# Attention on one core: the order of all engines as a table in the source, in place of a forward model

## The chip, the cores and the metric

The kernel runs on one core of a Trainium2 chip. Its time is the device time of one execution in microseconds; 113.61 us is the median of three executions before the change (113.47 to 114.02). A profile was taken of one more execution.

Engines are named as the profile names them: PE is TensorE (PEld its weight loads), DVE is VectorE, ACT is ScalarE, POOL is GpSimd, SP is SyncE, which here only issues transfers. Each engine works off its own queue in order; between engines there are semaphores.

## The reference

Plain softmax attention over 8 x 8 heads of 512 positions by 64:

```python
def reference(q, k, v):
    scale = 1.0 / np.sqrt(q.shape[-1])
    scores = np.einsum('bhqd,bhkd->bhqk', q, k) * scale
    scores = scores - scores.max(axis=-1, keepdims=True)
    attn = np.exp(scores)
    attn = attn / attn.sum(axis=-1, keepdims=True)
    return np.einsum('bhqk,bhkd->bhqd', attn, v).astype(np.float32)
```

q, k and v are (8, 8, 512, 64) in float32, normally distributed.

## The kernel before

**Tiling.** The 64 heads are taken two at a time: 32 pairs g, with the heads h = 0 and 1 (a and b below). A pair's q, k and v are loaded by one transfer of 256 KB each into float32 tiles, seven tiles deep for each of the three. POOL casts them to fp16 (`cast`, lines 511 to 526): v into one of twelve buffers with a column of ones, q and k into one of five `qkp` tiles. For pair 1's q alone the cast is shared: VectorE does the first half of it (line 523) and POOL the second (line 524).

**Stages of a pair.** TensorE turns k and q round in two halves (`transposes`, line 550; the part 0 is k, the part 1 is q), and VectorE copies the result from PSUM into `tqk` (`copy`). For pair 1 each half has a copy of its own (line 565), and the copy of the key half is issued inside `transposes`, at its end (line 560); for all other pairs one copy serves both halves (line 571). Then come the scores: a group m is two blocks of 128 keys by 512 queries in one of three score banks (`scores`, line 576, matmuls on line 598). There are 129 groups, four to a pair, with the last one cut in two halves. ScalarE takes the exponential of a group in one activation of 128 x 1024 (line 602). Sixteen groups (`ON_DVE`) are not given to ScalarE: VectorE computes their exponential with a "raise" out of the score bank (line 625) and five "passes" in SBUF (lines 642 to 665, called passes 0 to 4 here). Such a raise frees the score bank, which the group three further on takes.

**Values.** A value unit is a product of 128 queries of one head with its four blocks of keys (`values`, line 696, matmuls on line 704), with 65 columns: the last is the sum for the division. Seven units share a bank of PSUM. VectorE takes reciprocals of the sums (line 671) and multiplies (line 676) into a ring of 112 units, from which SP stores one or two heads at a time (lines 690 and 694). The two PSUM banks x0 and x1 are shared by the units and the transposes.

**What sets the order.** The kernel is written with a manual schedule: whatever the source issues first for an engine comes first in that engine's queue. The class `Plan` (lines 18 to 426) is a forward model: it steps a clock by 5 ns, keeps modelled times for each engine, the PSUM banks, the loads and the port that VectorE's passes and POOL's casts share, and by rules of urgency picks the next step of each engine. `run` returns the steps in the order of modelled time, and a loop at the end of the kernel issues them. Two things are added as waits: `cast_behind` (line 539) makes a cast wait for an earlier VectorE instruction, counted back from the latest one (`behind`), and before a cast of k a POOL memset of one number waits for transposes five pairs back. Twelve activations (`KNOWN`) wait for a cast six casts back.

The first pair is issued by hand (`first_pair`), ahead of the modelled steps: its activations are those on line 801.

Of the kernel before, what the change touches and what calls it, by code (L numbers as in the profile page):

```python
# [17 lines left out]
class Plan:  # L18

    SLOT, EXP, EXP_DONE, EXP_FIXED = 216, 853, 181, 64  # L20
    INTO, OUT_OF = 96, 96
    TRANSPOSE, V_UNIT = 222, 128
    TO_ACT, TO_DVE, TO_PE = 220, 210, 60

    COPY, NORM, RAISE = (601, 690), (50, 133), (1132, 1215)
    RECIPROCAL = 115
    SCALE, PRODUCT, EXTRA = 333, 600, 29
    COPY_1 = (400, 190)
    NORM_COLUMN, PASS_DONE = 67, 115
    PASSES = (SCALE, SCALE, PRODUCT, SCALE, PRODUCT)  # L30
    BITS = 2
    NEEDS = (None, None, 0, 2, 3)
    FIRST_EXP = 5000
    STEP = 5
    CALM, KEEN = 9000, 4
    FIRST_UNIT = 4
    KNOWN, OVER = (13, 15, 18, 20, 22, 24, 27, 42, 50, 61, 69, 97), 6
    ON_DVE = (5, 10, 16, 25, 28, 39, 44, 54, 63, 66, 74, 81, 91, 96, 103, 116)

    LATE_NORM, LATE_COPY, HURRY, SOON, BACKLOG = 700, 1500, 800, 160, 600  # L40
    LATE_MUL, WAIT = 400, 200
    SLACK, AHEAD = 0, 2

    CAST, CAST_PORT, CAST_DONE, TO_POOL = 557, 475, 130, 150
    SCALE_PORT, PRODUCT_PORT, GAP, REACH = 271, 537, 20, 5
    FIRST_LAND, LOAD, STORE, LATENCY, ISSUE = 5200, 752, 376, 2300, 470
    QUEUED, URGENT = 3500, 16
    PAIRED, STORE_ISSUE = 18, 520
    RAW, QK16, NV, NU = 7, 5, 12, 112
    PAIR, DUEK, DUEV, DUEL, PRE = 3300, 3550, 6000, 5000, 0  # L50

    def __init__(self, groups, pairs, first):
        self.groups, self.pairs = groups, pairs
        self.pe, self.act, self.dve = 7000, self.FIRST_EXP, 6300
        self.pool, self.port, self.dma = 4600, 4600, self.FIRST_LAND
        self.m, self.tiled = first, True
        self.read = []
        self.exps = {}
        for m in range(first):
            self.act += self.EXP + self.EXP_FIXED  # L60
            self.exps[m] = self.act + self.EXP_DONE
            self.read.append(self.exps[m])
        self.tq = {0: 5800}
        self.transposed = {0: 5800}
        self.next_t = 1
        self.part_t = 0
        self.banks = [5100, 5800]
        self.todo = [(g, h) for g in range(pairs) for h in range(2)]
        self.last = self.todo.pop()
        self.last_part = 0  # L70
        self.head = None
        self.units = self.FIRST_UNIT
        self.member = {b: m for m, grp in enumerate(groups) for b in grp}
        self.ready = []
        self.passes = []
        self.passed = {}
        self.raised = set()
        self.steps = []
        self.busy_dve = 0
        self.order, self.paired = [], 0  # L80

        late = {grp[0][0] for m, grp in enumerate(groups) if m in self.ON_DVE}
        due = []
        for g in range(pairs):
            scores = 5000 + self.PAIR * g
            if g:
                due += [(scores - self.DUEK, g, "k"), (scores - self.DUEK + 10, g, "q")]
            due.append((scores + self.DUEV + (self.DUEL if g in late else 0), g, "v"))
        self.due = sorted(due)
        self.uncast = list(self.due)  # L90
        self.casts = []
        self.landed, self.cast_done = {}, {}
        self.first_loads = [(g, n) for _, g, n in self.due if g < self.RAW]
        self.first_loads += [(self.RAW, "k"), (self.RAW, "q")]
        for x in self.first_loads:
            self.dma += self.LOAD
            self.landed[x] = self.dma
        self.loads, self.stores, self.stored = [], [], []
        self.sp = 1650 + 470 * len(self.first_loads)

    def note(self, t, *what):
        self.steps.append((t, len(self.steps)) + what)

    def trigger(self, t):

        ops = self.ops
        if not ops or ops[-1][1] <= t - 300:  # L110
            return 1, None
        n = len(ops) - 1
        while (
            n > 0
            and len(ops) - n < self.REACH
            and not ops[n][2]
            and ops[n][0] - ops[n - 1][1] <= self.GAP
        ):
            n -= 1
        if n > 0 and ops[n][0] - ops[n - 1][1] <= self.GAP:  # L120
            n -= 1
        return len(ops) - n, ops[n][1]

    def emit(self, t, back, after):
        _, g, n = self.uncast.pop(0)
        shared = (g, n) == (1, "q")
        self.note(t, "cast", g, n, back if t > self.CALM else 0)
        if not shared:
            self.casts.append((g, n, t if after is None else after + self.TO_POOL))
        if g + self.RAW < self.pairs:  # L130
            self.loads.append((g + self.RAW, n))

    def fits(self, t, soon=0):
        if not self.uncast:
            return False
        _, g, n = self.uncast[0]
        if n != "v" and g >= self.QK16 and self.transposed.get(g - self.QK16, 1e9) > t:
            return False
        return self.landed.get((g, n), 1e9) <= t + soon

    def step_pool(self, t):
        if self.uncast and self.uncast[0][1:] != (1, "q") and not self.casts and self.pool <= t:
            quiet = not self.passes and self.port <= t and not any(x[1] == "raise" for x in self.ready)
            if self.fits(t) and (quiet or self.uncast[0][0] - self.PRE < t):
                self.emit(t, 1, None)
        if self.casts and self.pool <= t and self.port <= t:
            g, n, after = self.casts[0]
            if after <= t and self.landed.get((g, n), 1e9) <= t:
                self.casts.pop(0)
                begin = max(self.pool, self.port, after, self.landed[(g, n)])  # L150
                self.pool = begin + self.CAST
                self.port = begin + self.CAST_PORT
                self.cast_done[(g, n)] = begin + self.CAST + self.CAST_DONE

    def step_sp(self, t):
        if self.sp > t or (self.loads and self.dma > t + self.QUEUED):
            return
        urgent = len(self.stores) > self.URGENT
        if self.loads and not urgent:
            g, n = self.loads[0]  # L160
            if self.cast_done.get((g - self.RAW, n), 1e9) <= t:
                self.loads.pop(0)
                self.note(t, "load", g, n)
                self.dma = max(self.dma, t + self.LATENCY - self.LOAD) + self.LOAD
                self.landed[(g, n)] = self.dma
                self.sp = t + self.ISSUE
                return
        if self.stores and self.stores[0] <= t:
            both = self.both()
            if both and (len(self.stores) < 2 or self.stores[1] > t):  # L170
                return
            heads = 2 if both else 1
            self.note(t, "store", heads)
            self.dma = max(self.dma, t + self.LATENCY - heads * self.STORE) + heads * self.STORE
            for _ in range(heads):
                self.stores.pop(0)
                self.stored.append(self.dma)
            self.paired += heads - 1
            self.sp = t + self.STORE_ISSUE

    def both(self):

        n = len(self.stored)
        g, h, u = self.order[n]
        return (
            self.paired < self.PAIRED
            and g < self.pairs - 2
            and h == 0
            and n + 1 < len(self.order)
            and self.order[n + 1][0] == g  # L190
            and u % self.NU + 8 <= self.NU
        )

    def room(self, t, u):
        heads = (u - self.NU - self.FIRST_UNIT + 3) // 4
        return heads <= 0 or len(self.stored) >= heads and self.stored[heads - 1] <= t

    def free(self, n=0):
        m = self.m + n
        if m >= len(self.groups):  # L200
            return 1e9
        g = self.groups[m][0][0]
        return max(0 if m < 3 else self.read[m - 3], self.tq.get(g, 1e9))

    def for_dve(self, m):
        return m in self.ON_DVE
# [692 lines left out]
```

## Time and profile before

| | us |
|---|---|
| median of the three executions | 113.61 |
| the profiled execution, whole | 113.92 |
| its span (first to last instruction) | 112.1 |
| ACT busy | 105.5 |
| PE busy | 103.2 |
| DVE busy | 100.8 |
| POOL busy | 65.9 |

The profile is of one execution, on the one core. A busy time is the union of an engine's instructions. The text quotes these views: the page's busy shares; the stage view (a stretch of time, its length, and for each engine its busy time and number of instructions, then the granted clock, the DMA share and GB/s); the list of waits (who waited for whom, us in total, how often, the longest); and the timeline (start in us, duration in us, engine, line, operation, what it writes and reads, and in brackets the idle time of the engine before it and what ended it). The line numbers are those of the kernel before.

In short: ScalarE, VectorE and TensorE are all busy for nine tenths of the time. Loads run at about 350 GB/s up to 80 us.

### The profile page before, as it was taken

The numbers are of one execution on the slowest core, as the hardware profiler recorded it, in microseconds if no ns is written. First come the engines' busy times: TensorE is split into PE (matmuls) and PEld (weight loads), VectorE is DVE, ScalarE is ACT, GpSimd is POOL, SyncE is SP. The second block draws the span as 40 slices with busy tenths as digits, with TensorE's granted clock in tenths as the row PEclk, the third lists the DMA queues.
The fourth block names the chain that finished last, engine by engine and source line by source line (L and its number), as shares of the span: only waits on it lengthen the run. The fifth ranks groups of instructions, "written<-read, shape, count | busy, mean of one in ns | idle before, by whom it ended". The sixth has DMA issues, their size and how long they took to land.

```text
span 112.1 us, 4408 instructions
## 1 busy us (share of the span) xinstructions
PE 103.2 (92%) x1728; PEld 69.4 (62%) x1728; DVE 100.8 (90%) x227; ACT 105.5 (94%) x118; POOL 65.9 (59%) x127
## 2 busy tenths in 40 slices
PE   7978889999799998999989999899999999999980
PEld 7634555766367766658647767577557577675660
DVE  1647999999999999999999999999999999997390
ACT  4599999999999999999999999999999999999970
POOL 2147768549756886495594786876784855600000
PEclk9999999999999999999999999999999999999997
DMA  3999999999999999999999999999999974142354
GB/s 106 276 359 353 345 350 347 355 336 349 345 347 336 341 346 343 354 364 375 370 358 382 350 355 377 354 372 362 343 366 305 349 245 143 52 141 99 97 167 161
DMA packets 35093, 33.84 MB, mean 302 GB/s; under 512 B 2304, under 2 KB 35072, under 8 KB 35072
## 3 DMA queue, kind: packets, MB, share of 16 engines
q1 hardware_dynamic: 34496, 33.04, 90.4%
q10 hardware_dynamic: 576, 0.52, 1.4%
q8 instruction: 13, 0.21, 0.8%
q14 instruction: 8, 0.07, 0.2%
HBM read 25.17 MB, written 8.39 MB: 299 GB/s over the span
## 4 chain that ended last, share of the span: by engine, by line
DVE 39%; PE 24%; DMA 15%; issue 8%; POOL 7%; SPq 3%; ACT 2%; POOLq 0%; ACTq 0%
PE o L704 13%; DMA v<-in_v_dram 10%; PE st L598 8%; DVE pd L625 8%; DVE tqk L571 7%; DVE ring L676 7%; DMA q<-in_q_dram 5%; DVE m L659 4%; POOL qkp L525 4%; DVE pd L665 4%; POOL vp L515 3%; PE tp L558 2%; SPq L509 2%; DVE m L642 2%; DVE pe L651 2%
## 5 line engine op out<-in xcount | busy, mean ns | idle before, releaser
L602 ACT ACTIVATE pt<-st 128x1024 f16<-128x1024 f32 (+1 forms) x110 | 100.3, 1144 | 0.2 <-PE st L598 0.2
L704 PEld LDWEIGHTS <-pt 128*128 128x128 f16 x880 | 38.8, 98 | 12.1 <-issue 10.2
L704 PE MATMUL o<-vp,pt 128*128 128x65 f16 x880 | 45.3, 194 | 0.4 <-POOL vp L515 0.2
L598 PE MATMUL st<-tqk 64*128 64x512 f16 (+1 forms) x250 | 41.7, 380 | 2.6 <-ACT pt L602 1.4
L525 POOL CAST qkp<-k 128x512 f16<-128x512 f32 x31 | 22.2, 717 | 11.3 <-DVE rc L671 5.3
L525 POOL CAST qkp<-q 128x512 f16<-128x512 f32 x30 | 21.7, 725 | 9.0 <-DVE rc L671 5.3
L515 POOL CAST vp<-v 128x512 f16<-128x512 f32 x32 | 21.4, 679 | 9.2 <-PE st L598 2.4
L676 DVE TENSOR_TENSOR ring<-o,rc 128x448 f32<-128x448 f32 (+2 forms) x37 | 22.3, 606 | 0.4
L704 PE MATMUL o<-vp,pe 128*128 128x65 f16 x128 | 21.8, 194 | 0.0
L704 PE MATMUL o<-vp,pd 128*128 128x65 f16 x128 | 21.7, 192 | 0.0
L558 PE MATMUL tp<-ident,qkp 128*128 128x128 f16 x248 | 19.6, 220 | 1.6 <-DVE tqk L571 0.8
L558 PEld LDWEIGHTS <-qkp 128*128 128x128 f16 x248 | 14.4, 97 | 9.9 <-issue 4.6
L571 DVE COPY tqk<-tp 128x1024 f16<-128x1024 f16 x30 | 20.3, 683 | 0.0
L625 DVE TENSOR_SCALAR pd<-st 128x1024 uint16<-128x1024 f32 x16 | 19.5, 1216 | 0.7 <-PE st L598 0.7
L598 PEld LDWEIGHTS <-tqk 64*128 64x128 f16 x250 | 10.7, 93 | 11.8 <-issue 4.6
L704 PEld LDWEIGHTS <-pe 128*128 128x128 f16 x128 | 12.5, 98 | 3.4 <-issue 3.3
L704 PEld LDWEIGHTS <-pd 128*128 128x128 f16 x128 | 12.5, 98 | 0.0
L659 DVE TENSOR_TENSOR m<-m 128x1024 f16<-128x1024 f16 x16 | 11.0, 685 | 0.0
L665 DVE TENSOR_TENSOR pd<-pd,m 128x1024 f16<-128x1024 f16 x16 | 10.9, 684 | 0.0
L671 DVE RECIPROCAL rc<-o 128x7 f32<-128x7 f32 (+2 forms) x37 | 7.4, 199 | 2.6 <-PE o L704 2.4
L661 DVE TENSOR_SCALAR m<-m 128x1024 f16<-128x1024 f16 x16 | 6.7, 418 | 0.1
L651 DVE TENSOR_SCALAR pe<-pd 128x1024 uint16<-128x1024 uint16 x16 | 6.6, 411 | 0.0
(51 smaller groups left out, 34.9 us busy)
## 6 DMA issues: line engine op xcount, KB each, us to landing
v<-in_v_dram SPq DMA_DIRECT2D x32, 256.0 KB, 5.8
k<-in_k_dram SPq DMA_DIRECT2D x31, 256.0 KB, 5.8
q<-in_q_dram SPq DMA_DIRECT2D x31, 256.0 KB, 5.9
out_dram<-ring SPq DMA_DIRECT2D x18, 256.0 KB, 5.5
out_dram<-ring SPq DMA_DIRECT2D x25, 128.0 KB, 2.2
k<-in_k_dram ACTq DMA_DIRECT2D x2, 128.0 KB, 2.8
q<-in_q_dram SPq DMA_DIRECT2D x2, 128.0 KB, 2.6
out_dram<-ring ACTq DMA_DIRECT2D x2, 128.0 KB, 1.9
```

Source lines behind the costliest of these rows:

```text
L515: return nc.gpsimd.tensor_copy(out=vps[g % NV][:, :, :, 0:D], in_=raw[g]["v"][:, :, :, :])
L525: return nc.gpsimd.tensor_copy(out=dst, in_=src[:, :, :, :])
L558: reads[g] = nc.tensor.transpose(tps[g][:, n, i, :], qkp[g][:, n, i, :], ident)
L571: nc.vector.tensor_copy(out=tqk[g][:, :, :], in_=tps.pop(g).rearrange("p n i c -> p n (i c)"))
L598: nc.tensor.matmul(st[:, x, cols], kc, qc[:, cols], start=True, stop=True)
L602: ins = nc.scalar.activation(out=pt[:, :, cols], in_=st[:, :, cols], func=EXP, scale=scale, bias=SHIFT)
L625: nc.vector.tensor_scalar(out=r["pd"][:, :, :], in0=r["st"][:, :, :], scalar1=BITS, scalar2=BIAS, op0=AluOp.mult, op1=AluOp.add,)
L651: ins = nc.vector.tensor_scalar(out=r["pe"][:, :, :], in0=u[:, :, :], scalar1=0x7C00, scalar2=None, op0=AluOp.bitwise_and,)
L659: ins = nc.vector.tensor_tensor(out=m16, in0=m16, in1=m16, op=AluOp.mult)
L665: ins = nc.vector.tensor_tensor(out=u16, in0=u16, in1=m16, op=AluOp.mult)
L676: nc.vector.tensor_tensor(out=ring[:, u % NU : u % NU + n, :], in0=o[:, x : x + n, 0:D], in1=rcs.pop(u)[:, 0:n].broadcast_to([P, n, D]), o ...
L704: nc.tensor.matmul(os[u // 7][:, u % 7, :], part[:, y * P : (y + 1) * P], vps[g % NV][:, h, c, :], start=(n == 0), stop=(n == len(parts) - 1),
```

## The change

The class `Plan` goes. In its place stands a class `Order` with strings: one letter for each step of all engines in program order, and lists that say which pair, head or bank each letter means. `ON_DVE`, `KNOWN`, the number of buffers, the first loads, the first pair and the functions that issue instructions stay, but for small things: the tiles of a VectorE group are now taken at its raise and not at its scores, and the shared cast of 1q counts among the instructions that a cast can be anchored to.

The letters: S scores, T half a pair's transposes, V a value unit, L a part of the last head, C copy, N reciprocal, M product, R raise, F the end, K cast, G load, w and W a store of one or two heads, and small letters for the passes. In `CASTS` a number behind the name is the count back to the VectorE instruction that the cast waits for; a name without one has no such wait.

```diff
-class Plan:
+class Order:
...
+    STEPS = (
+        "KTKSTKCSKSTRKSTSKCVVVNaSGSKMVGTcVVGTbVVGCSKSGRKTSKTdSKCSeTTfSKCSKRVVVKSVVNVgSKMSVhGTVTGk"
...
+    HEADS = (
+        "0a 0b 1a 1b 3a 3b 2a 2b 5a 5b 4a 4b 6a 6b 8a 8b 7a 7b 10a 10b 9a 9b 12a 11a 11b 14a 12b "
...
+    CASTS = (
+        "1k 1q 2k 2q 0v 3k 3q2 4k2 4q 5k 5q 1v2 6q 3v 6k2 2v2 7k3 7q2 9k 5v 6v 8k 8q2 10q11 9q2 "
+        "10k 4v2 8v 11k 11q2 12k 13k 12q 16q2 7v 14q 10v 13q 14k2 9v 16k 15k3 15q 11v 14v 12v "
+        "17q2 17k4 19q2 15v 18k 20k7 18q 19k 17v 13v 20q2 21k2 23k 21q 22q 22k 16v 21v2 19v 24q3 "
+        "23q 18v3 20v 24k 25k 26k 22v 25q 27q 26q 27k2 25v 28k 29k 23v2 28q 30k3 29q2 30q 24v 26v "
+        "30v 27v2 31v 31q 31k 29v 28v"
+    )
+    FIRST = "1k 1q 2k 2q 0v 3k 3q 4k 4q 5k 5q 1v 3v 6k 6q 2v 5v 4v 6v 7k 7q"
+    LOADS = (
+        "8k 9q 8q 9k 10k 13k 10q 10v 11q 8v 14q 15k 16q 15q 11k 14k 11v 12k 12q 9v 7v 17q 17k 15v "
...
+    def steps(self):
...
+        for step in self.STEPS:
+            if step == "S":
+                yield "scores", m, m in self.ON_DVE
+                m += 1
+            elif step == "T":
+                yield "transposes", g, part, int(self.BANKS_T[g - 1])
+                g, part = g + part, 1 - part
...
+            elif step == "K":
+                yield "cast", *next(casts)
...
-            nc.vector.tensor_copy(out=dst[:, :, 0:2], in_=src[:, :, 0:2])
+            dve(nc.vector.tensor_copy(out=dst[:, :, 0:2], in_=src[:, :, 0:2]))
...
-        if behind and latest:
-            tc.add_manual_dep(ins.ins, latest[behind - 1].ins.name, SYNC, reason="SBUF ports")
+        if behind:
+            tc.add_manual_dep(ins.ins, trail[-behind].ins.name, SYNC, reason="SBUF ports")
...
     def raise_(m):
         r = raised[m]
+        for n in ("pe", "pd"):
+            r[n] = dpool.tile([P, 2, S], U16, tag=n, name=f"{n}_{m}")
...
-        plan = Plan(groups, NP, 3)
-        steps = plan.run()
+        order = Order()
...
-        for what, *args in steps:
+        for what, *args in order.steps():
             do[what](*args)
```

More of the change, by code (lines that the diff above doesn't have):

```diff
@@ L1 @@
 import math
+import re
 from contextlib import ExitStack
@@ L463 @@
     dpool = ctx.enter_context(tc.tile_pool(name="pd", bufs=4))
-    wpool = ctx.enter_context(tc.tile_pool(name="work", bufs=Plan.BITS))
+    wpool = ctx.enter_context(tc.tile_pool(name="work", bufs=2))
     opool = ctx.enter_context(tc.tile_pool(name="out", bufs=4))
@@ L535, in dve @@
     def dve(ins):
-        latest[:] = [ins] + latest[: Plan.REACH]
+        trail.append(ins)
         return ins
     def cast_behind(g, name, behind):
-        if name == "k" and g - Plan.QK16 in reads:
+        if name == "k" and g - Order.QK16 in reads:
             small = nc.gpsimd.memset(mark[0:1, :], 0.0)
-            tc.add_manual_dep(small.ins, reads[g - Plan.QK16].ins.name, SYNC, reason="tile")
+            tc.add_manual_dep(small.ins, reads[g - Order.QK16].ins.name, SYNC, reason="tile")
         ins = cast(g, name)
         behind_it.append(ins)
-        if behind and latest:
-            tc.add_manual_dep(ins.ins, latest[behind - 1].ins.name, SYNC, reason="SBUF ports")
+        if behind:
+            tc.add_manual_dep(ins.ins, trail[-behind].ins.name, SYNC, reason="SBUF ports")
     def transposes(g, n, bank):
@@ L581, in scores @@
         if on_dve:
-            tiles = {n: dpool.tile([P, 2, S], U16, tag=n, name=f"{n}_{m}") for n in ("pe", "pd")}
-            raised[m] = {"st": st, **tiles}
-            parts = [tiles[n].bitcast(FP16) for n in ("pe", "pd")]
+            raised[m] = {"st": st}
         elif half == 1:
@@ L598, in scores @@
             nc.tensor.matmul(st[:, x, cols], kc, qc[:, cols], start=True, stop=True)
-            blocks[(g, c, h)] = [part[:, x, :] for part in parts] if on_dve else [pt[:, x, :]]
+            if not on_dve:
+                blocks[(g, c, h)] = [pt[:, x, :]]
         if on_dve:
@@ L604, in scores @@
         )
-        if m in Plan.KNOWN:
-            tc.add_manual_dep(ins.ins, behind_it[-Plan.OVER].ins.name, SYNC, reason="cast")
+        if m in KNOWN:
+            tc.add_manual_dep(ins.ins, behind_it[-OVER].ins.name, SYNC, reason="cast")
     FIRST, LINEAR, CUBIC = 0.4580331, 1.0167876, 0.1665620
@@ L623, in raise_ @@
         r = raised[m]
+        for n in ("pe", "pd"):
+            r[n] = dpool.tile([P, 2, S], U16, tag=n, name=f"{n}_{m}")
+        for x, b in enumerate(groups[m]):
+            blocks[b] = [r[n].bitcast(FP16)[:, x, :] for n in ("pe", "pd")]
         dve(
@@ L638, in pass_ @@
             r["m"] = wpool.tile([P, 2, S], U16, tag="m", name=f"m_{m}")
-        u, m16 = r["pd"], r["m"].bitcast(FP16)[:, :, :]
+        u = r["pd"]
         u16 = u.bitcast(FP16)[:, :, :]
+        if s != 1:
+            m16 = r["m"].bitcast(FP16)[:, :, :]
         if s == 0:
@@ L691, in store @@
             return
-        left = 2 * NP - 1 - (u0 + NI - Plan.FIRST_UNIT) // NI
+        left = 2 * NP - 1 - (u0 + NI - Order.FIRST_UNIT) // NI
         queue = nc.scalar if left < 2 else nc.sync
@@ L842 @@
     with tc.manual_schedule():
-        plan = Plan(groups, NP, 3)
-        steps = plan.run()
+        order = Order()
         first_loads()
-        for g, name in plan.first_loads:
+        for g, name, _ in order.read(order.FIRST):
             load(g, name)
```

434 lines of the change are left out of this document (60 added, 374 removed), and 5 rows, old and new, of tables (HEADS, LOADS).

## The prediction

> **What bounds the kernel now.** I read the page's busy shares first, then the stages, then what each engine waited for, then single instructions at the places where the new table differs.
>
> From the page, and then the stage view over the time from the activation at 9.21 us to the end of the last one (columns: length of the stage, busy us and count of each engine):
>
> ```profile
> span 112.1 us, 4408 instructions
> PE 103.2 (92%) x1728; PEld 69.4 (62%) x1728; DVE 100.8 (90%) x227; ACT 105.5 (94%) x118; POOL 65.9 (59%) x127
> ```
>
> ```profile
> 9.21:108.49 99.28, 95.57 (x1636) 64.05 (x1632) 96.03 (x200) 99.28 (x109) 62.80 (x117) 1.00 0.95 310
> ```
>
> ScalarE is busy for 99.28 of 99.28 us. It runs one exponential after the other, 109 of them, without a hole. The list of DVE groups stays the same sixteen in the change, so ScalarE gets the same exponentials, and what it does can't become shorter. Its only waits in the whole run are these:
>
> ```profile
> ACT L767 <- PEq L883: 1.7, 1, 1.7
> ACT q L769 <- DMA q<-in_q_dram: 0.6, 1, 0.6
> ACT pt L801 <- PE st_0a L794: 0.4, 1, 0.4
> ACT pt L602 <- PE st L598: 0.2, 1, 0.2
> ```
>
> The first three belong to the first pair, which the change doesn't touch. So an order can win back 0.2 us at most, 0.2%. It can lose without limit: whatever holds the scores back by more than ScalarE's lead is added to the end, once, and nothing after it can catch up.
>
> The second engine is VectorE:
>
> ```profile
> 9.43:103.06 93.63, 90.17 (x1525) 60.30 (x1524) 93.21 (x192) 93.63 (x103) 62.58 (x117) 1.00 0.98 321
> ```
>
> 93.21 of 93.63 us: it has 0.4 us of idle time before its last large job. It feeds ScalarE indirectly: a score bank that VectorE reads (the raise) has to come free for the scores three groups on. One example, the raise of group 28, the scores of group 31 and their activation:
>
> ```profile
> 27.52 1.22 DVE L625 TENSOR_SCALAR pd<-st 128x1024 uint16<-128x1024 f32 x1
> ```
>
> ```profile
> 28.79 0.39 PE L598 MATMUL st<-tqk 64*128 64x512 f16 x2 [0.52 <-DVE pd L625]
> ```
>
> ```profile
> 29.33 1.14 ACT L602 ACTIVATE pt<-st 128x1024 f16<-128x1024 f32 x1
> ```
>
> TensorE waited for the end of that raise, and the scores were done at 29.18, 0.15 us before ScalarE took them. At such places VectorE may be about 0.15 us late, no more.
>
> **The change, part by part.** I read both orders as lists of steps per engine. The counts are equal (126 scores, 62 halves of transposes, 252 value units, 94 casts, 73 loads in the loop, 45 stores, 202 VectorE steps), so no engine gets more work; only positions and waits differ.
>
> *1. The start of pair 1.* This is the largest term. Before, the steps are cast 1k, cast 1q, scores 3, transposes 1.0, cast 2k, transposes 1.1, copy 1. The table begins K T K S T K C: transposes 1.0 now stands ahead of cast 1q. For pair 1 the function `transposes` also issues the copy of the half it made (line 560), on VectorE, and the cast of 1q has a half on VectorE too (line 523). VectorE's queue therefore turns from cast, copy, copy into copy, cast, copy. The rows of before:
>
> ```profile
> 7.37 0.29 DVE L523 CAST qkp<-q 128x256 f16<-128x256 f32 x1 [1.15 <-DMA q<-in_q_dram]
> 7.76 0.42 DVE L565 COPY tqk<-tp 128x512 f16<-128x512 f16 x1
> ```
>
> ```profile
> 7.32 0.94 PE L558 MATMUL tp<-ident,qkp 128*128 128x128 f16 x8 [0.44 <-POOL qkp L525]
> 8.78 0.82 PE L598 MATMUL st<-tqk 64*128 64x512 f16 x6 [0.52 <-DVE tqk L565]
> ```
>
> ```profile
> 8.30 0.42 DVE L565 COPY tqk<-tp 128x512 f16<-128x512 f16 x1
> ```
>
> ```profile
> 9.21 2.90 ACT L602 ACTIVATE pt<-st 128x1024 f16<-128x1024 f32 x3 [0.18 <-PE st L598]
> ```
>
> Before, the cast ran at 7.37, hidden while the key transposes ran. In the new order the key copy stays at 7.76, since its transposes can't start before 7.32, and ends at 8.18. The cast, 0.29, then ends at about 8.4. The query transposes need it: eight transposes took 0.94, so four take 0.4 to 0.5, to about 8.85. The second copy, 0.42, ends at about 9.3 where it ended at 8.72. The scores that waited for it (0.52 us idle in the row) move from 8.78 to about 9.35, and the activation at 9.21, which is already one that ScalarE waits for, to about 9.78. **ScalarE loses about 0.57 us; I take 0.55.** Scores 3, which move behind transposes 1.0, need half of the 0.94 first and come to about 7.8 to 8.0, just when ScalarE gets to them: nothing. Ends: 0.4, if the steps overlap more than I let them; 0.7, if the cast now meets the 2k cast on POOL, which ran at this time.
>
> *2. Casts without an anchor.* Before, a cast waits for a VectorE instruction chosen so that it runs beside work that reads PSUM; by the planner's rule 5 of the 94 have no such wait. In the table 65 have none: they start when the cast before them is done. What a collision costs, in the one place of before where a pass clearly starts inside a running cast, with an undisturbed pass of the same form under it:
>
> ```profile
> 12.00 0.57 DVE L651 TENSOR_SCALAR pe<-pd 128x1024 uint16<-128x1024 uint16 x1
> 12.49 0.67 DVE L659 TENSOR_TENSOR m<-m 128x1024 f16<-128x1024 f16 x1
> ```
>
> ```profile
> 11.56 0.72 POOL L525 CAST qkp<-q 128x512 f16<-128x512 f32 x1 [0.23 <-DVE rc L671]
> ```
>
> ```profile
> 30.19 0.42 DVE L651 TENSOR_SCALAR pe<-pd 128x1024 uint16<-128x1024 uint16 x1
> 30.52 0.69 DVE L659 TENSOR_TENSOR m<-m 128x1024 f16<-128x1024 f16 x1
> ```
>
> From start to next start 0.49 against 0.33, 0.16 us lost to a cast that had been running 0.44 us. The other way round, when the pass is first, the cast waits:
>
> ```profile
> 36.10 0.61 POOL L515 CAST vp<-v 128x512 f16<-128x512 f32 x1
> ...
> 37.81 0.61 POOL L515 CAST vp<-v 128x512 f16<-128x512 f32 x1
> ...
> 38.78 1.01 POOL L525 CAST qkp<-k 128x512 f16<-128x512 f32 x1 [0.33 <-DVE ring L676]
> ```
>
> The cast at 38.78 takes 1.01 in place of 0.61, and VectorE loses nothing.
>
> The Trainium skill, SBUF — State Buffer, Who interferes with whom, says that GpSimd and such VectorE operations share a port pair as an exclusive lock: "Whoever issues first gets the shared pair for the whole instruction; the other **fully blocks** (not throttle)". Both rows agree in kind; by the page a pass that starts early in a cast would wait for nearly all of it, which no row of before shows.
>
> How often? The longest run of free casts in the table is eight behind one anchored cast: 18v, then 20v 24k 25k 26k 22v 25q 27q 26q. Casts chained without a wait follow each other at 0.57 us, three steps in the rows from 36.10 to 37.81. So nine casts fill about 5.1 us, in which VectorE's list has five passes (74's last three, 81's first two). Price of each: nothing when the pass is first, 0.16 by the row, more when it starts earlier in the cast. I take 0.10, between nothing and the row and nearer the row: VectorE 0.5 us late there, less the 0.15 of ScalarE's lead. **Estimate 0.35 us**, ends 0 and 4 (below).
>
> *3. Everything else, at nothing.* Scores are moved by up to eight value units against their neighbours, most of them earlier; that waits for nobody as long as the bank is free, and the later ones move where ScalarE's lead was over 0.8 us. The bound is 0.4 us, if one of them meets a bank that is not free. Loads are reordered thoroughly on SP's queue, and stores start earlier between them. Before, casts wait for a load only in the first 12 us:
>
> ```profile
> POOL qkp L525 <- DMA k<-in_k_dram: 3.2, 2, 3.0
> POOL qkp L525 <- DMA q<-in_q_dram: 0.8, 1, 0.8
> ```
>
> so transfers are well ahead. The one place where I see a late one: cast 9k stands ahead of 5v, 6v and 8k, and 9k's load is fourth behind 7q instead of third, some 0.75 us later. Four chained casts then end about 0.6 us after the transposes want them. The 0.55 of the start covers it; without that cover it costs up to 0.6 itself. Tiles taken at the raise, and the planner gone from the source, cost nothing on the chip.
>
> **The sum.** For the profiled execution (113.92, of which 112.1 is the span): 113.92 + 0.55 + 0.35 = 114.82. It lies 0.31 above the median of the runs shown, 113.61, so the forecast for the median is **114.5**.
>
> **The rivals.**
> - *The start alone (not slower).* The table's runs of casts fit the stretches between passes, each pass is first, and only the start is paid: 113.61 + 0.55 = 114.16, within 0.5%. For it: in the first half the runs fit well (11q, 12k, 13k, 12q stand beside a product, a raise and a copy in a row). Against it: nothing holds a free cast back when VectorE is 0.1 us late. It decides at 0.02 us of further loss, so it is a near thing. With the smaller slip of 0.4 it is 114.0.
> - *Casts ahead of the passes everywhere.* Laying the table's VectorE steps end to end with the rows' lengths, and the free casts 0.57 apart behind their anchors, about twenty passes start inside a cast. At 0.16 to 0.25 each that is 3 to 5 us, all of it on the raises, whose slack is 0.15: 113.61 + 0.55 + 3 = 117 and more. For it: VectorE's 0.4 us of idle time. Against it: near ties of a few hundredths, decided either way. The skill's rule of the full block speaks for this one.
> - *A small gain.* If the slip of the start were hidden and the 0.2 us won: 113.4. The copy of the key half can't pass the cast in one queue, so I see no way to it, and none at all to 0.57 us.
>
> **How the numbers follow.** A measurement of this kernel can tell about 0.5%, 0.57 us, from no change; the three runs before spread over 0.55. Forecast (start and some collisions, 114.2 to 115.3): 0.46. Start alone or less (113.3 to 114.17): 0.30. Casts ahead everywhere (over 115.3): 0.21. Gain over 0.5%: 0.03. Slower over 0.5%: 0.46 + 0.21 = 0.67. Range: from 113.8, which takes in most of the start-alone case, to 116.2, which takes in the lower half of the collisions; about 0.2 is left out. The forecast's own range is 114.2 to 115.3.
>
> **What would show it.** Step 1: on VectorE copy, cast, copy of pair 1, and an activation near 9.8 us with a wait of 0.7 or more. Step 2: passes longer than 0.45, and a wait of scores on raises after 70 us, in ScalarE's waits. Step 3: no cast that waits for a load past 26 us. I am wrong if the activation still starts at 9.2, if ScalarE has holes in places where neither a raise nor the start stands before them, or if the end grows behind the last activation.

## The result, and the profile after

The changed kernel takes 119.19 us in the median of four executions, the kernel before 113.65 beside it (113.47 to 114.02). The ratio is 1.048 with an interval of 1.0445 to 1.0514, so the change costs 5.5 us. The forecast was 114.5, with a range from 113.8 to 116.2. Three of the four executions took 119.06 to 119.24; the fourth, the one profiled, took 121.63 at a lowered clock, so the profile shown here is of one more execution, of 119.58 us, with the clock at 1.00.

From the page of that profile, where before stood a span of 112.1, VectorE (DVE) at 100.8 and ScalarE (ACT) at 105.5:

```profile
span 117.8 us, 4339 instructions
PE 105.8 (90%) x1728; PEld 70.1 (60%) x1728; DVE 106.5 (90%) x227; ACT 107.3 (91%) x118; POOL 64.5 (55%) x127
```

The numbers of instructions on the engines are the same. VectorE is busy 5.7 us longer, which is the growth of the span. The list of waits of ScalarE (us in total, times, longest), of which before only 0.2 us stood behind scores:

```profile
ACT pt L285 <- PE st L280: 3.7, 8, 0.7
ACT L456 <- PEq L571: 1.7, 1, 1.7
ACT pt L490 <- PE st_0a L483: 0.5, 1, 0.5
ACT q L456 <- DMA q<-in_q_dram: 0.5, 1, 0.5
ACT q L458 <- DMA q<-in_q_dram: 0.3, 1, 0.3
```

The new waits are for scores, but for some tenths at the first loads. Where VectorE's time went is in the view of groups, by line (busy us, then mean ns of one). The five passes before, then the five passes of the changed kernel, in the same order 0 to 4:

```profile
L642 DVE TENSOR_SCALAR m<-pd 128x1024 uint16<-128x1024 uint16 x16 | 6.5, 408 | 0.0
L651 DVE TENSOR_SCALAR pe<-pd 128x1024 uint16<-128x1024 uint16 x16 | 6.6, 411 | 0.0
L659 DVE TENSOR_TENSOR m<-m 128x1024 f16<-128x1024 f16 x16 | 11.0, 685 | 0.0
L661 DVE TENSOR_SCALAR m<-m 128x1024 f16<-128x1024 f16 x16 | 6.7, 418 | 0.1
L665 DVE TENSOR_TENSOR pd<-pd,m 128x1024 f16<-128x1024 f16 x16 | 10.9, 684 | 0.0
```

```profile
L331 DVE TENSOR_SCALAR m<-pd 128x1024 uint16<-128x1024 uint16 x16 | 7.6, 476 | 0.0
L340 DVE TENSOR_SCALAR pe<-pd 128x1024 uint16<-128x1024 uint16 x16 | 8.5, 534 | 0.0
L348 DVE TENSOR_TENSOR m<-m 128x1024 f16<-128x1024 f16 x16 | 11.4, 712 | 0.0
L350 DVE TENSOR_SCALAR m<-m 128x1024 f16<-128x1024 f16 x16 | 6.9, 434 | 0.0
L354 DVE TENSOR_TENSOR pd<-pd,m 128x1024 f16<-128x1024 f16 x16 | 12.4, 778 | 0.0
```

The sums are 41.7 and 46.8 us: 5.1 us more for the same eighty passes. Copies, raises and products did not grow. Singly, 64 of the passes last as before (within 0.06), and 16 last 0.15 to 0.44 longer, 5.54 us together. Before there was one such pass, with 0.16. Below, a pass that is longer than 0.41 (passes 0 and 1), 0.42 (pass 3) or 0.68 (passes 2 and 4) is called held, by the difference.

**A stretch of VectorE and POOL.** This is the run of nine casts from 18v to 26q that the prediction counted, from its fourth cast on. VectorE first, then POOL (x2 and x3 are casts joined in one row):

```profile
76.17 0.81 DVE L350 TENSOR_SCALAR m<-m 128x1024 f16<-128x1024 f16 x1
76.90 0.19 DVE L360 RECIPROCAL rc<-o 128x7 f32<-128x7 f32 x1
77.13 0.62 DVE L365 TENSOR_TENSOR ring<-o,rc 128x448 f32<-128x448 f32 x1
77.67 0.88 DVE L354 TENSOR_TENSOR pd<-pd,m 128x1024 f16<-128x1024 f16 x1
78.47 0.68 DVE L255 COPY tqk<-tp 128x1024 f16<-128x1024 f16 x1
79.08 0.79 DVE L331 TENSOR_SCALAR m<-pd 128x1024 uint16<-128x1024 uint16 x1
79.78 0.83 DVE L340 TENSOR_SCALAR pe<-pd 128x1024 uint16<-128x1024 uint16 x1
...
81.20 0.61 DVE L365 TENSOR_TENSOR ring<-o,rc 128x448 f32<-128x448 f32 x1
```

```profile
76.10 0.61 POOL L209 CAST qkp<-k 128x512 f16<-128x512 f32 x1
...
77.40 0.61 POOL L199 CAST vp<-v 128x512 f16<-128x512 f32 x1
77.96 2.37 POOL L209 CAST qkp<-q 128x512 f16<-128x512 f32 x3
```

The pass at 76.17 starts 0.07 after a cast. The cast ends at 76.71, 0.54 later, and the pass is held by 0.81 - 0.42 = 0.39. The pass at 77.67 finds 0.34 of a cast left (to 78.01) and is held by 0.20. In both, the hold is the rest of the cast less 0.14. The product at 77.13 and the copy at 78.47, which read PSUM, run beside casts at their usual length. The passes at 79.08 and 79.78 meet the second and third of the joined casts and are held by 0.38 and 0.42. Four passes lose 1.39 us here.

**How that reaches ScalarE.** The product at 81.20, late by these holds, frees the PSUM bank that the next transposes take, and these stand ahead of scores in TensorE's queue. TensorE, then ScalarE:

```profile
81.96 0.38 PE L242 MATMUL tp<-ident,qkp 128*128 128x128 f16 x4 [0.81 <-DVE ring L365]
82.28 0.39 PE L280 MATMUL st<-tqk 64*128 64x512 f16 x2
```

```profile
82.77 2.06 ACT L285 ACTIVATE pt<-st 128x1024 f16<-128x1024 f32 x2 [0.73 <-PE st L280]
```

The transposes wait 0.81 for the product (`ring`), the scores come at once behind them, and ScalarE has been idle for 0.73 when it gets them.

Behind the start ScalarE has seven holes. Three came this way (before its activations at 51.41, 82.77 and 100.36), and in TensorE's list of waits they are the first line below. At 69.63 the transposes waited for a reciprocal behind a held pass, and at 103.67 value units ahead of the scores had waited for a copy behind two held passes. The two small holes, of 0.18 and 0.17, were not followed. Scores that wait for a raise, the second line, stand in the list of before alone:

```profile
PE tp L242 <- DVE ring L365: 1.6, 3, 0.8
```

```profile
PE st L598 <- DVE pd L625: 0.7, 2, 0.5
```

### The profile page after: what moved, and what is told of

Its sections match the earlier page's. It is cut to its first block, busy times and chain, and to the rows that moved or that the text cites. A ratio compares the mean times of both kernels' runs of the same rounds, so it can differ in the third digit from the quotient of the medians.

```text
span 119.9 us, 4339 instructions
## 1 busy us (share of the span) xinstructions
PE 107.1 (89%) x1728; PEld 70.5 (59%) x1728; DVE 107.2 (89%) x227; ACT 108.2 (90%) x118; POOL 64.9 (54%) x127
## 4 chain that ended last, share of the span: by engine, by line
DVE 39%; DMA 27%; PE 18%; issue 6%; POOL 6%; SPq 1%; ACT 1%; POOLq 0%
DMA v<-in_v_dram 9%; PE o L393 9%; DMA k<-in_k_dram 8%; DVE tqk L255 8%; DVE ring L365 7%; PE st L280 6%; DMA q<-in_q_dram 5%; DMA out_dram<-ring 5%; DVE m L348 4%; DVE pd L354 4%; DVE pd L312 4%; DVE m L331 4%; DVE pe L340 3%; PE tp L242 3%; POOL qkp L209 3%
## 5 line engine op out<-in xcount | busy, mean ns | idle before, releaser
L285 ACT ACTIVATE pt<-st 128x1024 f16<-128x1024 f32 (+1 forms) x110 | 102.8, 1046 | 5.3 <-PE st L280 4.7
L393 PE MATMUL o<-vp,pt 128*128 128x65 f16 x880 | 48.1, 195 | 1.4 <-DVE tqk L255 1.1
L393 PEld LDWEIGHTS <-pt 128*128 128x128 f16 x880 | 40.0, 98 | 15.6 <-issue 13.2
L280 PE MATMUL st<-tqk 64*128 64x512 f16 (+1 forms) x250 | 42.7, 386 | 2.1 <-DVE tqk L255 0.7
L209 POOL CAST qkp<-k 128x512 f16<-128x512 f32 x31 | 21.6, 701 | 14.5 <-DVE rc L360 4.4
L209 POOL CAST qkp<-q 128x512 f16<-128x512 f32 x30 | 20.7, 699 | 12.8 <-DVE pe L340 3.6
L242 PE MATMUL tp<-ident,qkp 128*128 128x128 f16 x248 | 21.4, 223 | 4.4 <-DVE ring L365 1.6
L354 DVE TENSOR_TENSOR pd<-pd,m 128x1024 f16<-128x1024 f16 x16 | 12.5, 778 | 0.0
L340 DVE TENSOR_SCALAR pe<-pd 128x1024 uint16<-128x1024 uint16 x16 | 9.0, 561 | 0.0
L331 DVE TENSOR_SCALAR m<-pd 128x1024 uint16<-128x1024 uint16 x16 | 7.6, 477 | 0.0
```

Of the source, the lines that this page charges most:

```text
L209: return nc.gpsimd.tensor_copy(out=dst, in_=src[:, :, :, :])
L242: reads[g] = nc.tensor.transpose(tps[g][:, n, i, :], qkp[g][:, n, i, :], ident)
L280: nc.tensor.matmul(st[:, x, cols], kc, qc[:, cols], start=True, stop=True)
L285: ins = nc.scalar.activation(out=pt[:, :, cols], in_=st[:, :, cols], func=EXP, scale=scale, bias=SHIFT)
L340: ins = nc.vector.tensor_scalar(out=r["pe"][:, :, :], in0=u[:, :, :], scalar1=0x7C00, scalar2=None, op0=AluOp.bitwise_and,)
L354: ins = nc.vector.tensor_tensor(out=u16, in0=u16, in1=m16, op=AluOp.mult)
```

## The experiments

Four theories stood at the beginning: (1) the start of pair 1 costs its 0.57 us; (2) free casts get ahead of VectorE's passes and hold them; (3) loads and casts in another order come late; (4) the moved TensorE and VectorE steps cost something of their own. In what follows, "held" is summed over one profile, and the spans are those of the profiles.

**The changed kernel again.** No edit.

> The changed kernel again, for a profile with the clock undisturbed. All theories expect 119.15 (119.06 to 119.24, as its other runs). What tells them apart is in the profile: if casts that run into VectorE's passes cost the time (theory 2), the passes sum to 4 us or more above those of before (their mean there is 0.41 to 0.69 by form), 15 or more of the 80 passes start inside a running cast, and ScalarE's idle time is put down to scores that waited for raises. If late loads cost it (theory 3), casts wait for DMA for 2 us or more past 26 us. If the moved TensorE work costs it (theory 4), scores wait for nothing but stand behind value units.

It took 119.58, and its profile is the one above: 16 held passes with 5.54 us, as theory 2 has it. Scores did not wait for raises, though, but mostly for the chain just shown. Past 26 us one wait of a cast is put down to a load, 1.65 us at 69.29, by the cast of 21v; that cast also waits for a VectorE step, which ended 0.07 before it, at 69.22, so the load made it late by 0.07 at most. Before 26 us the cast of 9k, the one late load that the prediction named, waited 1.01 us for its load and started at 24.97; ScalarE ran from 9.80 to 38.41 without a hole all the same. Both speak against theory 3.

**The start exchanged back.**

```diff
-        "KTKSTKCSKSTR...
+        "KKTSTKCSKSTR...
```

> The changed kernel with one pair of steps exchanged: cast 1q stands ahead of the first transposes of pair 1 again. Theory 1 (the start costs its 0.57 and nothing later gives it back): 118.6, that is 0.5 to 0.6 less than the changed kernel's 119.15, with the activation of scores 4 at 9.2 to 9.3 us. Rival: the later lateness of VectorE is set by casts and not carried over from the start, so that the gain is eaten within some tens of us: 119.0 to 119.2.

The median is 119.23, of executions from 118.52 to 120.20: the times don't tell 0 from 0.6. The profile (118.92 us, span 117.1) has the same holes of ScalarE from 50 us on as that of the changed kernel (0.53, 0.17, 0.39, 0.72, 0.64, 0.46), each 0.66 earlier. But 0.29 of that was there from the first activation on (5.05 against 5.34, the arrival of a load), and 17 passes are held, with 5.88 us. The hole of 0.57 at 9.80 is gone: ScalarE runs from 7.83 to 50.22 in one row. But what is left of the gain at the end is within the spread, so this run doesn't decide on theory 1; the kernel before with the start alone and the last pair of kernels do.

**Every cast with a wait.**

```diff
+        if not behind and len(behind_it) > 5:
+            behind = 1
         if behind:
```

> The changed kernel with every cast from the sixth on made to wait for a VectorE step: those that have no wait of their own in the table wait for the VectorE step issued last before them. Order unchanged on every engine. Theory 2 (free casts start ahead of passes and hold VectorE's port): 4 to 5 us come back less what the waits cost, 114.2 to 116. Theory 3 (loads in another order) and theory 4 (scores and values in another order): 118.5 to 119.5, since no load and no matmul is moved. If the anchors fit worse than those of before, so that casts come late for transposes, it is above 119.5.

123.2, ratio 1.082 (1.076 to 1.089): slower by 4, outside what theory 2 gave; only the last sentence of the expectation had allowed for it. Its profile tells why. 19 passes are still held, with 5.03 us. And casts come late, so that VectorE waits; one place on POOL, TensorE and VectorE (line numbers behind the edit are two higher here):

```profile
15.41 0.74 POOL L209 CAST qkp<-q 128x512 f16<-128x512 f32 x1 [1.17 <-DVE pd L314]
```

```profile
16.20 0.40 PE L244 MATMUL tp<-ident,qkp 128*128 128x128 f16 x4 [1.19 <-POOL qkp L209]
```

```profile
16.64 0.69 DVE L257 COPY tqk<-tp 128x1024 f16<-128x1024 f16 x1 [0.96 <-PE tp L244]
```

The cast is bound to the raise that was issued last. It starts only when that raise, beside which it could have run, is over; the transposes come 1.19 late, and VectorE stands idle for 0.96 in front of its copy. From 9.43 us to its last step VectorE is idle for 6.5 us, where before had 3.1. The added holds, the added idle time and the later start (9.71 for 9.21) are 4.9 + 3.4 + 0.5 = 8.8; the span grew by 121.2 - 112.1 = 9.1. A wait alone doesn't help: the place counts.

**The kernel before without the waits of its casts.**

```diff
-        if behind and latest:
-            tc.add_manual_dep(ins.ins, latest[behind - 1].ins.name, SYNC, reason="SBUF ports")
```

> The kernel before with the order of every engine as it was, and no cast waiting for a VectorE step any more. Theory 2: casts run as soon as their load is there and the tile is free, so that passes start inside casts as in the changed kernel, 3 to 6 us slower: 117 to 119.5. Theories 3 and 4, by which the anchors carry little: 113.4 to 114.2.

127.99, ratio 1.126 (1.119 to 1.133), more than theory 2 gave. With the order of before on all engines 42 passes are held, with 14.5 us, for a span of 125.9, 13.8 more. Passes 1 and 4 in the view of groups:

```profile
L649 DVE TENSOR_SCALAR pe<-pd 128x1024 uint16<-128x1024 uint16 x16 | 9.9, 619 | 0.0
L663 DVE TENSOR_TENSOR pd<-pd,m 128x1024 f16<-128x1024 f16 x16 | 13.4, 838 | 0.0
```

**The kernel before with the start alone.**

```diff
         steps = plan.run()
+        late = ("cast", 1, "q", 0)
+        steps.remove(late)
+        steps.insert([x[:3] for x in steps].index(("transposes", 1, 0)) + 1, late)
```

> The kernel before with only the start of the table: cast 1q stands behind the first transposes of pair 1, all else as it was. Theory 1 (VectorE runs copy, cast, copy; the activation of scores 4 slips from 9.21 to 9.8): 0.5 to 0.65 slower, 114.2 to 114.5, since ScalarE has nothing to give it back with. Rival (the slip is absorbed by the 0.15 us that other steps have in hand): 113.5 to 114.0.

114.44 against 113.86, ratio 1.0064 (1.0024 to 1.0104): 0.58 us, as theory 1 has it, with an interval from 0.3 to 1.2. In its profile the activation starts at 10.02 and not at 9.8, since the first copy was already 0.23 later (7.99 where before had 7.76).

**Thin casts, in the kernel before and in the changed one.** The same edit in both, cut to the casts of q and k (the casts of v are cut alike, v 0 to 7 are filled at the start, and the five `qkp` tiles become fixed ones):

```diff
-        return nc.gpsimd.tensor_copy(out=dst, in_=src[:, :, :, :])
+        if g < 6:
+            return nc.gpsimd.tensor_copy(out=dst, in_=src[:, :, :, :])
+        return nc.gpsimd.tensor_copy(out=dst[:, :, 0:1], in_=src[:, :, 0:1, :])
```

> The kernel before with thin casts, as the control for the next one. It leaves work out: from pair 6 on a q or k cast converts a quarter of its tile, and so do the casts of v but those of pairs 8 to 11; the rest of the fp16 tiles keeps what was in them, and the tiles of v 0 to 7 are filled with ones at the start. Its casts already run beside steps that read PSUM, so that shorter ones change nothing: 113.4 to 114.2 by every theory, the upper part if the longer fill at the start delays the first casts.

> The changed kernel with the same thin casts (from pair 6 on a q or k cast converts a quarter of its tile, and so do the casts of v but those of pairs 8 to 11; the rest keeps what was in it). Orders, waits, loads and matmuls are those of the changed kernel. Theory 2 (passes wait for the rest of a running cast): a cast of a quarter of the length leaves next to nothing to wait for, so that only the start's 0.57 remains over the control: 114.0 to 114.8. Theories 3 and 4 (late loads, moved TensorE work): 118 to 119.3, since all of that is as it was.

The control took 115.92, above what was expected: filling eight tiles of v at the start held VectorE until 5.3 us, and ScalarE's first activation waited 2.25 (2.34 in the other kernel). The changed kernel with thin casts took 118.16 in the median of three executions (117.31 to 118.74; a fourth took 120.07). By the number alone that lies in the range of theories 3 and 4, but the control is 2 us up too, and only the distance from it counts: 2.2 us in these medians, 116.0 - 114.1 = 1.9 in the spans, where full casts have 5.5 and 5.7. The 0.57 expected was missed as well, since a cast of a quarter still takes 0.29 us where nothing holds it up, in place of 0.61. Ten passes are held, with 1.25 us, 1.09 more than in the control, and the start slips by 0.87. The two make 1.96, the 1.9 of the spans. So more than half of the loss goes with the length of the casts alone, orders and waits unchanged; theories 3 and 4 would have kept it.

**The last 39 casts laid out anew.** Each one was put where VectorE's list has steps that read PSUM, bound to the step after which these or the pass ahead of them begin, in the order in which they are needed. Cut to the core:

```diff
     CASTS = (
...
-        "... 19k 17v 13v 20q2 21k2 23k 21q 22q 22k 16v 21v2 19v 24q3 "
-        "23q 18v3 20v 24k 25k 26k 22v 25q 27q 26q 27k2 25v 28k 29k 23v2 28q 30k3 29q2 30q 24v 26v "
-        "30v 27v2 31v 31q 31k 29v 28v"
+        "... 19k 17v 13v1 20q1 21k1 21q1 22k1 22q1 19v1 16v1 23k1 23q1 24k1 24q1 "
+        "18v1 25k1 25q1 21v1 26k1 26q1 20v1 27k1 27q1 23v1 28k1 28q1 22v1 29k1 29q1 26v1 24v1 30k1 "
+        "30q1 27v1 31k1 31q1 25v1 28v1 29v1 30v1 31v1 "
```

> The changed kernel with the start exchanged back, and with its casts from 13v on (the last 39, from about 60 us) laid out anew: in the order in which they are needed, each waiting for a VectorE step such that it runs beside steps that read PSUM; the loads behind them follow that order. The steps of VectorE, TensorE and the stores stay as the table has them. Theory 2: of the 17 passes that waited for a cast in the changed kernel with its start exchanged, 12 stood past 60 us, with 4.3 us; these go, and the five before stay: 118.5 less 4 is 114.3 to 114.9. Theory 4 (moved scores, values and passes): 118.2 to 118.8. If only a few of the twelve were on the path: 115.5 to 117.

116.75 (115.92 to 117.09), ratio 1.0236 (1.0183 to 1.0289): 2.5 less, not 4. The second half did what theory 2 says. One pass is held there, by 0.26; before this edit it was twelve with 4.3 us. ScalarE from 50 us on, first with the start alone exchanged back, then with the new layout:

```profile
50.75 16.64 ACT L285 ACTIVATE pt<-st 128x1024 f16<-128x1024 f32 x18 [0.53 <-PE st L280]
67.56 1.02 ACT L285 ACTIVATE pt<-st 128x1024 f16<-128x1024 f32 x1 [0.17 <-PE st L280]
68.97 12.42 ACT L285 ACTIVATE pt<-st 128x1024 f16<-128x1024 f32 x13 [0.39 <-PE st L280]
82.11 16.95 ACT L285 ACTIVATE pt<-st 128x1024 f16<-128x1024 f32 x18 [0.72 <-PE st L280]
99.70 2.85 ACT L285 ACTIVATE pt<-st 128x1024 f16<-128x1024 f32 x3 [0.64 <-PE st L280]
103.01 10.54 ACT L285 ACTIVATE pt<-st 128x1024 f16<-128x1024 f32 x12 [0.46 <-PE st L280]
```

```profile
51.24 16.60 ACT L285 ACTIVATE pt<-st 128x1024 f16<-128x1024 f32 x18 [0.53 <-PE st L280]
68.00 42.53 ACT L285 ACTIVATE pt<-st 128x1024 f16<-128x1024 f32 x47 [0.15 <-PE st L280]
```

The same 65 activations take 62.8 us (50.75 to 113.55) and 59.3 (51.24 to 110.53): 3.5 us gained, of 4.0 in holds. In the untouched first half the holds are the same 1.6 us in both, but they fell differently: here a cast of 6k got ahead of a pass at 19.40 (held by 0.42), and ScalarE has a hole of 0.58 at 21.33; the other had a hold of 0.28 at 18.03 and no hole. This was the fastest of the four executions. What the slower three lost, and why the median is 1.9 us above the 114.9 expected, stays open.

**All casts from pair 6 on laid out anew.** The same for 82 of the 94, and with it loads in the order of the casts; once with the start exchanged back, once with the start of the change.

> The changed kernel with the start exchanged back, and with all casts from pair 6 on (82 of 94) laid out anew as in the run of the second half: in the order in which they are needed, each waiting for a VectorE step so that it runs beside steps that read PSUM; loads follow the casts, the first loads of pairs 6 and 7 too. The order of VectorE's, TensorE's and SyncE's other steps is the table's. Theory 2: at most two or three passes start inside a cast, ScalarE's waits of over 0.3 us are gone, 113.4 to 114.4, that is no difference from the kernel before. Theory 4 (moved scores, values and passes cost something of their own): 115 to 117, with ScalarE's waits where no pass was held up. If my laying out is too late for some transposes of the first half: 114.5 to 116, with TensorE waiting for casts.

> The same with the start as in the change (the first transposes of pair 1 ahead of cast 1q). Theory 1: 0.5 to 0.65 above the run without it, as in the kernel before; the activation of scores 4 starts at 9.7 to 10.0. Rival: VectorE has some tenths in hand in the table's order, and the slip is gone by 30 us: 0 to 0.3 above.

The medians are 114.17 with the start of before, ratio 1.0047 (1.0019 to 1.0075), and 114.66 with that of the change, ratio 1.008 (1.0052 to 1.0107), against 113.92. In the first, two passes are held, with 0.33 us, and the span is 112.2. Its passes 1 and 4, and ScalarE's activations of the table as one row without a hole:

```profile
L340 DVE TENSOR_SCALAR pe<-pd 128x1024 uint16<-128x1024 uint16 x16 | 6.7, 421 | 0.0
L354 DVE TENSOR_TENSOR pd<-pd,m 128x1024 f16<-128x1024 f16 x16 | 10.9, 682 | 0.0
```

```profile
7.88 100.73 ACT L285 ACTIVATE pt<-st 128x1024 f16<-128x1024 f32 x110
```

The table's order of VectorE, TensorE and the stores thus costs 0.25 us in the medians (0.2 to 0.9 by the interval) and 0.1 in the spans; theory 4 can't explain 5.5 us. The two kernels differ by 0.49, near theory 1's size, though single executions of them overlap. The profiles are plainer. The scores of pair 1, first with the start of before, then with that of the change:

```profile
8.33 0.61 PE L280 MATMUL st<-tqk 64*128 64x512 f16 x4 [0.52 <-DVE tqk L249]
```

```profile
8.83 0.61 PE L280 MATMUL st<-tqk 64*128 64x512 f16 x4 [0.52 <-ACT pt L285]
```

They stand 0.50 apart, ScalarE waits 0.44 once behind the first pair and has no other hole to the end, and the spans differ by 0.5. So the slip is not given back, and theory 1's rival falls. The activation came at 9.26, not at the expected 9.7 to 10.0, because this execution was earlier as a whole: its first copy of pair 1 began at 7.23, the changed kernel's at 7.62. Neither kernel is faster than the kernel before.

**The same order, without the waits.** Casts and loads in the new order could themselves have been the cure (theory 3); so the first of the two was run with the waits of its 82 casts left out:

```diff
-        if behind:
+        if behind and len(behind_it) <= 12:
```

> The run with all casts laid out anew (114.17), orders of casts, loads and all else as there, but the 82 casts from pair 6 on wait for no VectorE step any more. Theory 2 in its strict form (it is the place in time of a cast beside VectorE that costs, not the order of casts and loads): casts start when load and tile allow, some 16 to 40 passes start inside one, at a mean of 0.34 us each 5 to 14 us: 119 to 128. Theory 3 (the order of casts and loads was what the new layout mended): 114.0 to 115.5.

126.06, ratio 1.107 (1.101 to 1.113): 35 held passes with 12.6 us, and a span 12.4 longer. Theory 3 falls: the order of casts and loads alone cures nothing, their place beside VectorE does. Well-placed waits in the table's own order of casts were not run.

Side by side, from the profiles:

| kernel | passes held | us held | span less 112.1 |
|---|---|---|---|
| before | 1 | 0.16 | 0 |
| before, the start alone | 1 | 0.16 | 0.7 |
| all casts laid out anew | 2 | 0.33 | 0.1 |
| the same, start of the change | 2 | 0.34 | 0.6 |
| last 39 laid out anew | 6 | 1.8 | 2.0 |
| changed | 16 | 5.5 | 5.7 |
| changed, start exchanged back | 17 | 5.9 | 5.0 |
| changed, every cast with a wait | 19 | 5.0 | 9.1 |
| same new order, no waits | 35 | 12.6 | 12.4 |
| before, no waits | 42 | 14.5 | 13.8 |

The row with a wait for every cast is the one where holds don't account for the span: there VectorE stood idle.

## Why the prediction was wrong

**What bounds the kernel: right.** ScalarE had nothing to win and everything to lose, and what it lost came from VectorE. One point was off: the prediction let VectorE's lateness reach ScalarE "all of it on the raises". No scores waited for a raise in the changed kernel; the largest holes came through a product that freed a bank for transposes ahead of the scores. That is one of the signs of being wrong that the prediction had set: holes with neither a raise nor the start before them.

**Step 1, the start of pair 1: right, place and size.** VectorE's rows of the changed kernel, TensorE's and ScalarE's:

```profile
7.62 0.42 DVE L249 COPY tqk<-tp 128x512 f16<-128x512 f16 x1 [0.81 <-PE tp L242]
7.96 0.43 DVE L207 CAST qkp<-q 128x256 f16<-128x256 f32 x1
8.88 0.42 DVE L249 COPY tqk<-tp 128x512 f16<-128x512 f16 x1 [0.49 <-PE tp L242]
```

```profile
9.37 0.60 PE L280 MATMUL st<-tqk 64*128 64x512 f16 x4 [0.52 <-DVE tqk L249]
```

```profile
9.80 1.94 ACT L285 ACTIVATE pt<-st 128x1024 f16<-128x1024 f32 x2 [0.57 <-PE st L280]
```

Copy, cast, copy; the second copy at 8.88 (worked out: 8.85), the scores at 9.37 (9.35), the activation at 9.80 (9.78). The last hundredths are luck: the first copy started 0.14 earlier than set, and the cast took 0.43 where 0.29 was set, as the upper end had it, with the cast of 2k on POOL at that time. The wait is 0.57, not the 0.7 or more given as a sign. Taken alone the start measured 0.58 in the kernel before and 0.49 in the kernel laid out anew.

**Step 2, "casts without an anchor": the step that failed.** The mechanism was right, and both factors of its size were wrong: 5 passes at 0.10, less 0.15, stood for 16 passes at 0.35, 0.35 us for 5.4.

The price was read off one row, 0.16, as if it were the cost of any collision, and halfway to nothing it became 0.10. But it is one point of a line. That cast ran from 11.56 for 0.72 to 12.28, and the pass started at 12.00 with 0.28 of it left; 0.28 less 0.13 is 0.15. In six profiles (the changed kernel, its start exchanged back, every cast with a wait, the last 39 laid out anew, and the two without waits) 206 passes start inside the record of a cast, and 139 of them are held by more than 0.05 us. In nine of ten of these, the rest of the cast less the hold was between 0.128 and 0.142 us; the longest hold was 0.445. Of the other 67, 62 start in the last 0.18 us of the cast, and five within 0.06 of its start, where the cast waited in their place. A pass that starts at random in the 0.48 us in which it can be held would lose 0.24 in the mean; the 139 lost 0.33. The Trainium skill, SBUF — State Buffer, Who interferes with whom, has it that the loser waits for the whole instruction of the other. The runs agree with it to the last 0.13 us of the cast's record, and that was the sentence by which to read the row. Whether the cast lets go that early, or the pass needs the port only that long after its own start, the records don't tell.

The count was made in the longest run of free casts, and there it was good: four of the five passes named were held, by 1.39 us. But eleven others stood in shorter runs, at single free casts, or at a cast with a wait whose follower ran on into the next pass; one more was the collision that before had too. The laying end to end that found "about twenty" was in the text, as the rival "casts ahead of the passes everywhere", with 3 to 5 us and a chance of 0.21. Its count was the better one, and its price of 0.16 to 0.25 still too low. What spoke against it, "near ties of a few hundredths, decided either way", holds for single places only (the five passes above, or the one at 19.40): on the whole the ties fell against VectorE.

**Step 3, everything else at nothing: right in size**, by the kernel with all casts laid out anew (0.25 us over before in the medians, with the start of before) and by the loads: the late one that the prediction named came, and ScalarE did not feel it.

**The sum.** 0.57 for the start and 5.54 - 0.16 = 5.38 for the holds make 5.95; the spans differ by 5.7 and the medians by 5.5, so 0.2 to 0.4 was absorbed. That fits VectorE's idle time from 10 us to its last step, 3.1 us before and 2.6 in the changed kernel. On ScalarE's side the idle time grew by 3.7 us and the busy time by 1.8 (105.5 to 107.3) for the same activations. Where a new row of activations begins after a wait, the overlap of some 0.1 us with the one before it is lost; with eight waits this is part of the 1.8 only, and the rest was not followed up.

## What to carry to other kernels

Where a cast on GpSimd can start ahead of an SBUF pass on VectorE, cost the pass at the rest of that cast less 0.13 us, and count over the whole table, laid end to end, not over its worst run. A wait for the step issued last isn't enough where the cast stands at the wrong place in the order: in the layout that cured it each cast waits for the step issued last too, but stands where it then runs beside VectorE's work out of PSUM, after a pass that goes first. When VectorE has 0.4 us to spare in 94, held passes come out at the end nearly one for one.

## What was not expected of the hardware

- The hold follows a line with hardly any scatter: rest of the cast less 0.13 us, in 139 passes with a standard deviation of 0.007 us. By the records a pass is held when it starts in the first 0.48 of a cast's 0.61 us, but for five that started within 0.06 of the cast.
- Whether a kernel with many near ties varies more from one execution to the next is not shown. The changed kernel with its start exchanged back ran from 118.52 to 120.20, and the one with its last 39 casts laid out anew from 115.92 to 117.09; but the one with all casts laid out anew, with two held passes, ran from 113.91 to 115.41. What a tie can do shows at 19.40, where it came with a hole of 0.58.
- A cast of a quarter of the elements takes 0.29 us where nothing holds it up, in place of 0.61: nearly half. In the mean, with those that waited, it is 0.36 to 0.40 in place of 0.68 to 0.70. With thin casts the holds fell from 5.54 to 1.25 us, but at a quarter of the elements converted from pair 6 on.
